# Second layer's down-projection: eight more slots each for split weights and split activations, in the activations' dead tile

## The chip, the cores and the metric

The kernel runs on one core of one Trainium2 chip. The metric is the device time of one execution in microseconds (us). An execution of one program repeats within some tenths of a per cent; the median of a few is given. A profile is taken of one execution more, by the hardware profiler, and has a time of its own.

## The reference, cut to what matters

The program is one inference step of a two-layer encoder for 1152 rows (1024 of a prompt, 128 of eight samples), with d_model 1024. Each layer has attention, and a GEGLU MLP with a causal convolution of width 3 between the up-projection and the activation. What bears on this case is the end of the MLP, in the second layer:

```python
D_MODEL = 1024; D_FF = 2816
def conv_ffn(h, prev, w_up, conv_w, conv_b, w_down):
    u = h @ w_up
    ...
    a, g = jnp.split(y, 2, axis=-1)
    out = (jax.nn.gelu(g) * a) @ w_down      # (1152 x 2816) @ (2816 x 1024)
...
x = layer_norm(ALPHA * x + (1 + g_f) * f, ln_g[l, 1], ln_b[l, 1])
```

All inputs and results are float32.

## The kernel before

**Split operands.** A float32 operand is held as two tiles in the matmul's rounded type: hi, a cast of the value (ScalarE, `copy`, line 183), and lo, the value less hi (VectorE, `split`, line 194). A product is then three matmuls: lo by hi, hi by lo, hi by hi. A pair (hi, lo) lives in a slot; `Ring` hands the slots of a list out in turn, again and again. Before a slot is written anew, the last matmul that read it must be done.

**The second layer's down-projection** is `down2`, called at the end of `ffn` (for the first layer `down` is called in its place, which is not touched). The 22 blocks of 128 rows of the weight are taken as 11 pairs, m = 0 to 10, the even block e = 2m and the odd block o = 2m + 1. The prompt's product is computed by a scheme of Strassen's kind with seven block products in place of eight, in the order 1, 2, 5, 6, 3, 7, 4. Sums of activation blocks (`actS`) and of weight blocks (`wT`) were written to DRAM during the up-projection, the activations themselves to `actD`. `product(q, banks, ...)` runs one of the seven: for each m it calls `fetch`, which gives an activation (hi, lo) and a weight (hi, lo), and issues 4 x 3 matmuls (128 x 128 by 128 x 512, line 1603) into four banks of PSUM. In products 1, 2, 5 and 6 there are three more for the 128 sample rows into a bank of their own, so a step has 15 matmuls there and 12 in products 3, 7 and 4.

What `fetch` issues for a step:

- the activation (`act`): a load of 128 x 512 (line 1595), in products 1, 2, 5 and 6 another of 128 x 128 for the samples (line 1597), into the lo half of its slot; then the cast and the subtraction in place;
- the weight (`weight`): a load of 128 x 512 (line 1587) into a raw buffer, or, for `wT`, straight into the lo half of its slot; then cast and subtraction;
- product 5 loads two weight blocks (lines 1628 and 1629), takes their difference on GpSimd (line 1630) and splits both, so it takes two weight slots per step; product 6 too takes two, one for `wT` and one for a raw weight.

Raw buffers are rings of their own: nine (`early`) in products 1 and 2, six (`late`) in the others, eight (`diffs`) in product 5.

**The slots.** The weights' ring `subs` has six slots of 512 columns, halves of the tiles `wh` and `wl`. The activations' ring `acts` has seven slots of 640 columns in `X1` (named `xa` in the profile). `H` is a tile of 128 x 2 x 8 x 1152 (hi and lo, eight blocks of d_model, 1152 rows) which holds the up-projection's split activations; after the last matmul of the up-projection (line 1229) nobody reads them. Before the change, eight slots in H (columns 512 to 1024 of each block, `more`) join the weights' ring after product 6, for products 3, 7 and 4, and for product 4 the ring starts over at its first slot.

**Between the products** the banks are read out: by ScalarE copies (line 1722 after product 1, 1729 after product 5) and VectorE additions (1732 after product 6, 1749, 1756), with gates by line 1657. Product 2 adds on in product 1's banks, product 6 in product 5's, product 3 in product 6's. Meanwhile residual rows, gates and LN rows are loaded (1081, 970, 971, 978), and the rows' normalisation (`head`, `tail`, `norm_last`, lines 1001 to 1026) follows product 6 and runs to the end. The last six steps of product 4 are kept back (`KEEP`) and run bank by bank, so that the last rows can be finished one after another.

**Order.** No engine's order is written by hand. A planner runs through the program with simulated times and puts onto each engine's queue what is ready, earlier program lines first. All loads and stores are issued by SyncE's one queue (SP), in the planner's order. An instruction on the chip waits for the tiles it needs, and each engine's queue is worked off in order.

Of the kernel before, what the change touches and what calls it, by code (L numbers as in the profile page):

```python
# [36 lines left out]
NK = NFF // 2  # L37
# [68 lines left out]
class Trunk:  # L106
# [285 lines left out]
    def attention(self, l, wk):  # L392
# [5 lines left out]
        if l == 0:  # L398
            self.X1 = self.x1p.tile([128, 9216], F32R, name="xa", tag="x1")
        xa = Arena(self.X1)  # L400
        khi = [xa.take(1024) for _ in range(2)]
# [683 lines left out]
    def woload(self, l, i):  # L1085
        X1, X2 = self.X1, self.X2
        loc = ((5120, 6144), (7168, 8192), (0, 2048), (3072, 1024))
        loc = [tuple(X1[:, o : o + 1024] for o in p) for p in loc]
        loc = self.wslots[0:2] + loc + [self.wslots[2], (X1[:, 4096:5120], X2[:, 0:1024])]
        self.wo[i] = self.wload(self.I[("wo0", "wo1")[l]][i // 4, i % 4], el="ppppvvvv"[i], dst=loc[i])  # L1090
        return self.wo[i]
# [60 lines left out]
    def tviews(self):  # L1152
        X1, X2 = self.X1, self.X2
        TT = [(X1[:, 0:2304], X1[:, 2304:4608]), (X1[:, 4608:6912], X1[:, 6912:9216]), (X2[:, 0:2304], X2[:, 2304:4608])]
        return [[x.rearrange("p (k n) -> p k n", k=4) for x in t] for t in TT]
# [390 lines left out]
    def down2(self, l, xsrc, xdst, affs, act_sums):  # L1546
        nc, I, F, H = self.nc, self.I, self.F, self.H
# [26 lines left out]
        late = Ring(raws)  # L1574
        diffs = Ring([F[:, o : o + 512] for o in range(2048, 6144, 512)])
        subs = self.subslots(ws[1:4])
        X1 = self.X1
        acts = Ring([(X1[:, o : o + 640], X1[:, o + 640 : o + 1280]) for o in range(0, 8960, 1280)])
        more = [(H[:, 0, c, 512:1024], H[:, 1, c, 512:1024]) for c in range(8)]
        hfr = Ring([self.hf, self.gateS])  # L1580
        wdn, wT, actD, actS = I["wdn"][l], self.wT, self.actD, self.actS
        lo_half, hi_half = slice(0, 512), slice(512, 1024)
# [62 lines left out]
        def product(q, banks, bs=None, new=True, keep=0, hook=None):  # L1645
            for m in range(NK - keep):
                a, w, w2 = fetch(q, m)
                for i in range(4):
                    mm(self.bank(banks[i]), a, i, w, new and m == 0, m == NK - 1)
                if bs is not None:  # L1650
                    mm(self.bank(bs), a, 4, w2, q in (1, 5) and m == 0, q in (2, 6) and m == NK - 1)
                if hook:
                    hook(m)
# [81 lines left out]
        def tails(k):  # L1735
            def hook(m):
                if m in TAILS[k]:
                    t = TAILS[k][m]
                    tail(t)
                    rows(*{0: (3,), 1: (4, 5), 2: (6,), 3: (7,)}.get(t, ()))  # L1740

            return hook

        subs = Ring(subs.items + more)
        rings = Ring([zt]), Ring([self.hf])
        rows(8, 0)
        product(3, B, new=False, hook=tails(0))
# [9 lines left out]
            nc.vector.tensor_sub(q5[i], u4[i], q5[i])  # L1757
            gate(u4[i], u4[i], 4 + i, 1)
        keep = KEEP[l]
        subs = Ring(subs.items[0 : NK - len(more)] + more if l == 0 else subs.items)  # L1760
        product(4, E, keep=keep, hook=tails(2))
        kept = [(m, fetch(4, m)) for m in range(NK - keep, NK)]
        for i in range(4):
# [296 lines left out]
```

## Time and profile before

| | us |
|---|---|
| median of 3 runs | 2764.35 |
| lowest, highest run | 2763.35, 2785.1 |
| profiled execution | 2773.36 |
| its span, from the first to the last instruction | 2771.6 |
| mean granted TensorE clock in it | 0.985 |
| the stage's matmuls (line 1603), first to last start | 2487.7 to 2755.2 |

Times in the profile's rows are us from the start of the span. PE is TensorE's matmuls, PEld its weight loads, DVE VectorE, ACT ScalarE, POOL GpSimd, SP SyncE, which issues the DMAs; a "q" behind the name means the engine's queue. `PS` is PSUM, `wl` and `wh` the weight slots, `xa` the activation slots, `F`, `ws`, `w0f` and `x2f` other tiles in SBUF. A row of a waits view has the engine, line and tile that waited, what it waited for, the total in us, how often, and the longest. A row of a chain has start, length and what was going on. A row of a timeline has start, length, engine, line, operation, tiles and count, and in brackets the engine's idle time just before and what ended it.

### The profile page before, as it was taken

What the parts mean: (1) busy time and instruction counts of PE and PEld (TensorE: products, weight loads), DVE (VectorE), ACT (ScalarE), POOL (GpSimd) and SP (SyncE); (2) the same over time, 40 slices, a digit from 0 to 9 for tenths busy, and PEclk for the clock granted to TensorE, in tenths of its full rate; (3) what the DMA queues carried; (4) which work ended last, traced back from release to release, by engine and by line L of the source; (5) the groups of instructions that cost most, each with busy time, mean ns of one, the idle gap of its engine ahead of it and who ended that gap; (6) DMA issues with size and microseconds to landing.
All of it is one profiled execution on the core that took longest, in us unless ns stands there. A gap on an engine that the chain in (4) does not pass through costs nothing.

```text
span 2771.6 us, 47111 instructions
## 1 busy us (share of the span) xinstructions
PE 2654.1 (96%) x17266; PEld 2347.8 (85%) x17266; DVE 1928.0 (70%) x3836; ACT 1347.6 (49%) x2777; POOL 1063.8 (38%) x775
## 2 busy tenths in 40 slices
PE   7999889999999999999999999989999999999997
PEld 5987768989999998788898888867899999997776
DVE  4376768776667684867754677766787778785669
ACT  3475733433334343443436666663454454454454
POOL 3132523444434467664221121242466656632101
PEclk9999999999999999999999999999999999999999
DMA  8756534574444446765757457763445343347564
GB/s 295 232 160 187 152 105 167 163 238 150 139 157 152 143 140 221 243 213 183 273 199 264 112 164 193 217 203 129 167 139 184 135 143 130 136 152 240 191 222 156
DMA packets 229527, 498.27 MB, mean 180 GB/s; under 512 B 37456, under 2 KB 99232, under 8 KB 229296
## 3 DMA queue, kind: packets, MB, share of 16 engines
q1 hardware_dynamic: 229296, 495.27, 54.8%
q8 instruction: 136, 2.23, 0.3%
q14 instruction: 95, 0.78, 0.1%
HBM read 378.15 MB, written 126.47 MB: 182 GB/s over the span
## 4 chain that ended last, share of the span: by engine, by line
PE 36%; DVE 6%; DMA 4%; issue 2%; ACT 2%; POOL 1%; SPq 0%; DVEq 0%; ACTq 0%; POOLq 0%
PE PS L1229 15%; PE PS L1603 6%; PE PS L325 5%; PE PS L312 4%; PE PS L608 2%; PE PS L586 1%; DVE wl L194 1%; DMA xa<-actD 1%; PE PS L557 1%; DVE F L524 1%; PE PS L560 1%; DVE xa L194 1%; DMA w0f<-in_wdn_dram 1%; PE PS L735 1%; DMA xa<-actS 0%
## 5 line engine op out<-in xcount | busy, mean ns | idle before, releaser
L1229 PE MATMUL PS<-H,wh 128*128 128x256 f32 (+1 forms) x2288 | 351.6, 294 | 0.0
L1229 PEld LDWEIGHTS PS<-H,wh 128*128 128x128 f32 x2288 | 318.5, 189 | 0.4 <-issue 0.4
L1190 DVE TENSOR_TENSOR F<-PS,F 128x256 f32<-128x256 f32 (+1 forms) x446 | 196.9, 452 | 168.0 <-PE PS L1229 160.2
L183 ACT CAST wh<-F 128x512 fp32r<-128x512 f32 (+3 forms) x241 | 147.8, 624 | 214.2 <-PE PS L1229 101.5
L194 DVE TENSOR_TENSOR wl<-F,wh 128x512 fp32r<-128x512 f32 (+2 forms) x225 | 219.6, 987 | 44.3 <-ACT wh L183 42.9
L1229 PE MATMUL PS<-H,wl 128*128 128x256 f32 (+1 forms) x1144 | 201.4, 297 | 6.8 <-ACT F L1197 6.2
L1603 PE MATMUL PS<-wh,xa 128*128 128x512 f32 x584 | 189.2, 403 | 13.7 <-ACT wh L183 7.0
L1229 PEld LDWEIGHTS PS<-H,wl 128*128 128x128 f32 x1144 | 168.4, 189 | 12.9 <-ACT F L1197 6.4
L1229 PE MATMUL PS<-xa,wh 128*128 128x320 f32 (+1 forms) x1152 | 176.2, 294 | 0.0
L183 ACT CAST xa<-xa 128x384 fp32r<-128x384 f32 (+2 forms) x143 | 85.9, 604 | 172.4 <-DMA xa<-actD 143.8
L1229 PEld LDWEIGHTS PS<-xa,wh 128*128 128x128 f32 x1152 | 159.7, 188 | 0.4 <-issue 0.4
L1472 DVE TENSOR_TENSOR xa<-xa 128x384 fp32r<-128x384 f32 x66 | 98.9, 1511 | 77.4 <-ACT xa L183 77.4
L1603 PEld LDWEIGHTS PS<-wh,xa 128*128 128x128 f32 x584 | 112.2, 193 | 42.6 <-ACT wh L183 8.8
L646 POOL TENSOR_TENSOR F<-F,x2r 64x512 f32<-64x512 f32 x62 | 79.3, 1279 | 164.9 <-DVE F L622 149.8
L183 ACT CAST wh<-ws 128x512 fp32r<-128x512 f32 (+1 forms) x131 | 95.5, 736 | 95.1 <-PE PS L1229 40.9
L1349 POOL TENSOR_TENSOR F<-F 128x1152 f32<-128x1152 f32 x44 | 124.2, 2823 | 43.9 <-DVE F L1342 23.6
L325 PE MATMUL PS<-xa,H 128*128 128x512 f32 x504 | 132.5, 405 | 6.2 <-ACT xa L183 3.3
L312 PE MATMUL PS<-H,w0r 128*128 128x384 f32 (+1 forms) x720 | 137.4, 341 | 0.0
L1278 DVE SCALAR_TENSOR_TENSOR F<-F 128x1024 f32<-128x1024 f32 (+2 forms) x160 | 130.1, 863 | 4.3 <-ACT F L1317 3.3
L312 PE MATMUL PS<-H,wh 128*128 128x384 f32 (+1 forms) x672 | 131.3, 339 | 0.0
L586 PE MATMUL PS<-C,F 128*128 128x128 f32 x720 | 112.6, 280 | 14.7 <-DVE wh L593 5.8
L312 PEld LDWEIGHTS PS<-H,w0r 128*128 128x128 f32 x720 | 124.3, 188 | 2.8 <-issue 1.5
(354 smaller groups left out, 6885.9 us busy)
## 6 DMA issues: line engine op xcount, KB each, us to landing
ws<-in_adaw_dram SPq DMA_DIRECT2D x64, 512.0 KB
ws<-in_wup_dram SPq DMA_DIRECT2D x49, 512.0 KB
F<-in_adaw_dram SPq DMA_DIRECT2D x48, 512.0 KB
F<-in_wup_dram SPq DMA_DIRECT2D x39, 512.0 KB
actD<-F SPq DMA_DIRECT2D x33, 576.0 KB
ws<-in_wdn_dram SPq DMA_DIRECT2D x33, 512.0 KB
F<-in_wdn_dram SPq DMA_DIRECT2D x33, 512.0 KB
xa<-kH SPq DMA_DIRECT2D x60, 256.0 KB
```

The costliest lines, as they stand in the source:

```text
L183: nc.scalar.copy(out, in_)
L194: self.eng(el).tensor_sub(lo, src, hi.bitcast(F32))
L312: mm = self.nc.tensor.matmul(out[:, 0:n], w[a][:, k * 128 : k * 128 + 128], H[:, p, k, s0 : s0 + n], start=i == 0, stop=i == 23)
L325: self.nc.tensor.matmul(out[:, 0:n], H[:, p, j * kn + k, t0 : t0 + 128], w[a][:, k * n : k * n + n], start=i == 0, stop=i == 23,)
L586: nc.tensor.transpose(t[:, n * 128 : n * 128 + 128], p[:, (kt - k0) * 128 : (kt - k0) * 128 + 128], self.ident)
L646: self.eng("v" if last else "p").tensor_mul(on[r, q], on[r, q], rb[r, :])
L1190: nc.vector.tensor_add(d, v(ps), a if len(a.shape) == 3 else v(a))
L1229: self.pairmm = nc.tensor.matmul(ps[:, 0:m], w[a][:, k * 128 : k * 128 + 128], x(p, k, n), start=start and c == 0, stop=c == 11, skip_grou ...
L1278: nc.vector.scalar_tensor_tensor(o, u, cw[:, cc, i : i + 1], o, op0=ALU.mult, op1=ALU.add)
L1349: nc.gpsimd.tensor_mul(yg, yg, ya)
L1472: nc.vector.tensor_sub(lo, raw, hi.bitcast(F32))
L1603: self.downmm = nc.tensor.matmul(ps, a[p][:, i * 128 : i * 128 + 128], w[q], start=first and c == 0, stop=last and c == 2, skip_group_chec ...
```

## The change

The eight slots in H are taken from the start of the stage: the weights' ring has 14 slots in all seven products (6 as before, then columns 0 to 512 of each of H's eight blocks), the activations' ring has 15 (7 as before, then columns 512 to 1152 of each block). The two later changes of the weights' ring go: it isn't extended after product 6 and doesn't start over for product 4.

```diff
         subs = self.subslots(ws[1:4])
+        subs = Ring(subs.items + [(H[:, 0, c, 0:512], H[:, 1, c, 0:512]) for c in range(8)])
         X1 = self.X1
-        acts = Ring([(X1[:, o : o + 640], X1[:, o + 640 : o + 1280]) for o in range(0, 8960, 1280)])
-        more = [(H[:, 0, c, 512:1024], H[:, 1, c, 512:1024]) for c in range(8)]
+        acts = [(X1[:, o : o + 640], X1[:, o + 640 : o + 1280]) for o in range(0, 8960, 1280)]
+        acts = Ring(acts + [(H[:, 0, c, 512:1152], H[:, 1, c, 512:1152]) for c in range(8)])
...
-        subs = Ring(subs.items + more)
         rings = Ring([zt]), Ring([self.hf])
         rows(8, 0)
         product(3, B, new=False, hook=tails(0))
...
         keep = KEEP[l]
-        subs = Ring(subs.items[0 : NK - len(more)] + more if l == 0 else subs.items)
         product(4, E, keep=keep, hook=tails(2))
```

## The prediction

> **What bounds the kernel now.** I read the page first, for the engine shares and the chain, then the rows of the stage's one matmul line.
>
> ```profile
> span 2771.6 us, 47111 instructions
> PE 2654.1 (96%) x17266; PEld 2347.8 (85%) x17266; DVE 1928.0 (70%) x3836; ACT 1347.6 (49%) x2777; POOL 1063.8 (38%) x775
> PE 36%; DVE 6%; DMA 4%; issue 2%; ACT 2%; POOL 1%; SPq 0%; DVEq 0%; ACTq 0%; POOLq 0%
> L1603 PE MATMUL PS<-wh,xa x584: 387/394/795, 2487.7 to 2751.8; 128*128 128x512 f32 x195
> L1603 PE MATMUL PS<-wl,xa x292: 388/394/628, 2489.9 to 2751.6; 128*128 128x512 f32 x146
> L1603 PE MATMUL PS<-H,xa x180: 387/389/402, 2681.3 to 2755.2; 128*128 128x512 f32 x180
> ...
> L1229 PE MATMUL PS<-H,wh x2288: 276/304/468, 535.4 to 2494.2; 128*128 128x256 f32 x102, 128*128 128x320 f32 x89
> ```
>
> TensorE is the engine of the chain. In the L1603 rows (count, then shortest, median and longest duration in ns, then first and last start) the stage has 584 + 292 + 180 = 1056 matmuls and lasts from 2487.7 to 2755.2, 267.5 us; before 2681 none of them reads H. The up-projection (L1229) reads H for the last time at 2494.2.
>
> The next view cuts the stage into stretches: length, then busy time and instructions of PE, PEld, DVE, ACT and POOL, granted clock, DMA share, GB/s. I set the cuts where the 10 us rows of the same view had few matmuls.
>
> ```profile
> 2485.00:2500.00 15.00, 12.53 (x63) 9.76 (x63) 12.59 (x24) 10.08 (x19) 1.93 (x3) 1.00 0.66 214
> 2500.00:2530.00 30.00, 30.00 (x133) 24.62 (x132) 20.34 (x20) 10.82 (x18) 14.09 (x9) 1.00 0.95 295
> 2530.00:2545.00 15.00, 11.63 (x40) 8.98 (x39) 5.02 (x7) 7.38 (x13) 0.00 (x0) 0.77 0.60 202
> 2545.00:2605.00 60.00, 60.00 (x259) 48.60 (x258) 36.39 (x45) 24.39 (x40) 9.98 (x7) 1.00 0.57 177
> 2605.00:2640.00 35.00, 28.48 (x113) 21.74 (x112) 19.15 (x30) 19.29 (x34) 0.00 (x0) 0.95 0.59 189
> 2640.00:2660.00 20.00, 20.00 (x89) 16.43 (x88) 10.57 (x17) 9.04 (x16) 0.00 (x0) 1.00 0.60 204
> 2660.00:2670.00 10.00, 7.49 (x26) 5.68 (x26) 9.13 (x16) 5.08 (x9) 0.00 (x0) 0.83 0.51 168
> 2670.00:2750.00 80.00, 80.00 (x352) 65.53 (x351) 68.20 (x136) 42.89 (x70) 5.24 (x2) 1.00 0.64 218
> ```
>
> Undisturbed, 2545 to 2605 holds 259 matmuls in 60 us: 4.32 per us, 0.232 us each. 1056 of them would take 245 us, so the stage holds about 23 us that are not its matmuls (a little of it is the up-projection's last). That is the ceiling of what any buffering can give: 0.8% of the kernel. Three stretches miss matmuls. 2530 to 2545 should hold 64.8 and holds 40: 24.8 missing, **5.7 us**. 2605 to 2640 should hold 151 and holds 113: 38 missing, **8.8 us**. 2660 to 2670 should hold 43 and holds 26: 17 missing, **4.0 us**. Together 18.5 us; the rest, some 4 to 5 us, lies before 2500, in the handover from the up-projection. From 2670 on nothing is missing.
>
> What each of the three waits for is in the waits of each engine and in the chain between 2590 and 2664:
>
> ```profile
> PE PS L1603 <- DVE xa L194: 3.4, 1, 3.4
> PE PS L1603 <- DVE F L1732: 2.5, 1, 2.5
> ...
> 2524.49 0.38 SPq L1597 DMA_DIRECT2D xa<-actD  x1
> 2534.25 0.72 ACT L183 CAST xa<-xa 128x640 fp32r<-128x640 f32 x1 [5.96 <-DMA xa<-actD]
> ...
> 2610.62 4.18 DMA wl<-wT
> 2614.83 0.20 ACT wh L183
> 2618.47 5.18 DMA wl<-wT
> 2623.67 0.63 ACT wh L183
> 2627.96 5.59 DMA xa<-actD
> ...
> 2657.82 3.25 DMA w0f<-in_wdn_dram
> 2661.09 0.63 ACT H L183
> 2661.74 0.56 DVE H L194
> 2662.35 0.69 DVE F L1732
> ```
>
> The first stall is one activation load: issued at 2524.49, cast at 2534.25, 9.8 us later, right behind the 30 us in which DMA was 0.95 busy. The second is a run of loads of 4.2 to 5.6 us, each on the chain from issue to landing. The third is the eviction L1732, queued on DVE behind two splits of weights whose raw load was late.
>
> **The change part by part.** No arithmetic, DMA or matmul is added or taken away; what changes is how early a load or a split may start.
>
> *Weight slots, 6 to 14 in products 1, 2, 5, 6.* Products 5 and 6 use two slots per step of 15 matmuls, so six slots hold three steps: 3 x 15 x 0.232 = 10.4 us from a slot's release to its next use. In product 6 the wT load goes straight into the lo half of its slot and so can't start before the release. In that time must fit the wait on SP, the landing (4.2 to 5.2 us above), the cast and the subtraction, each behind what is queued on ACT and DVE:
>
> ```profile
> L183 ACT CAST xa<-xa 128x640 fp32r<-128x640 f32 x44 | 31.6, 728 | 62.6 <-DMA xa<-actD 51.6 <-PE PS L1603 3.8 <-issue 2.5
> L194 DVE TENSOR_TENSOR xa<-xa 128x640 fp32r<-128x640 f32 x44 | 38.6, 886 | 47.7 <-ACT xa L183 42.1 <-DMA xa<-actD 2.8 <-DMA F<-in_wdn_dram 2.7
> L194 DVE TENSOR_TENSOR wl<-F,wh 128x512 fp32r<-128x512 f32 x37 | 35.0, 968 | 3.5 <-ACT wh L183 3.5
> ```
>
> With 14 slots it is seven steps, 24.4 us. The chain's loads then start some 14 us sooner than they are needed, more than the longest landing in it. Bounds for the second stall: 0 to 8.8 us gone; I take 8, since its waits are short against the 14 us won.
>
> Can DVE follow? A step of product 5 costs it 0.886 + 2 x 0.968 = 2.82 us per 3.48 us of matmuls, and from 2545 to 2605 it was busy 36.39 of 60. It can, and it may begin product 5 while product 2 still runs. ACT is further from its limit.
>
> *Activation slots, 7 to 15.* A slot lasts one step, so the depth goes from 24 to 52 us. The first stall sits where seven slots were already deep enough on paper, so depth alone doesn't explain it: DMA was full at 295 GB/s. What the slots can do is bring loads forward into 2485 to 2500, where DMA was only 0.66 busy: 15 us x 0.34 x 295/0.95 GB/s is 1.6 MB, or five activation loads of 256 + 64 KB. Bounds: 0 to 5.7 us; I take 4.
>
> *The third stall.* No slot is short for L1732 itself. It goes if the two splits ahead of it on DVE have their data earlier. Bounds 0 to 4.0; I take 2.5, nearer to gone, because the loads of product 3 get the same lead as all others.
>
> About 2 us of its 4.0 are slow clock: granted 0.83 in that stretch, with matmuls 0.43 us apart after a wait of only 2.5 us.
>
> ```profile
> 2663.18 0.47 PE L1603 MATMUL PS<-wh,xa 128*128 128x512 f32 x1 [2.51 <-DVE F L1732]
> 2665.81 1.05 PE L1603 MATMUL PS<-wh,xa 128*128 128x512 f32 x2
> 2666.66 0.63 PE L1603 MATMUL PS<-wl,xa 128*128 128x512 f32 x1
> ```
>
> The Trainium skill, "TensorE: Matmul & The Clock Gate", in Part 1 on the HAM clock gate, puts the fall to half clock at an idle window of about 3.4 us; by that a 2.5 us wait should cost 2.5 us and not the 4.0 counted above, and the sum would be 1 to 1.5 us smaller. The spacing in the last two rows speaks against it here.
>
> *The new wait, and the start.* A load into H waits on SP for the up-projection's last matmul on that block; behind it in SP's one queue stand the first weights of product 1, and TensorE waits for those. Today's kernel has that wait too, for three loads of product 7, which now come later:
>
> ```profile
> 2493.78 1.32 SPq L1587 DMA_DIRECT2D H<-wT  x3
> ```
>
> They were issued within a microsecond of the block's release, 6 us after the stage's first matmul, so I count the wait itself at nothing; what it costs if it is misplaced is a rival below. The first six weights and seven activations lie where they lay, so the 4 to 5 us before 2500 stay. Splits of the later ones no longer wait for a matmul and can slip in between the last up-projection's evictions, where DVE is busy 12.59 of 15 us. Bounds: one split per engine lost twice, 2 us, down to nothing; I take 1 us lost.
>
> *Products 3, 7, 4.* They had 14 weight slots; they get no more. The last product's ring now runs on instead of starting over. Nothing is missing there after 2670, so I count 0. DVE hides this: 68.20 of 80 us busy. If the matmuls came faster than before, DVE would be late next, but they can't.
>
> **Sum:** 8 + 4 + 2.5 - 1 = 13.5 us. The profiled execution took 2773.36 us (span 2771.6, and 1.8 around it); it would become 2759.9. The median of the runs is 2764.35, 9 us lower for the same work, so the forecast is 2764.35 - 13.5 = **2751 us**.
>
> **The rivals.**
>
> *Slots were not the limit.* SP's longest waits between 2485 and 2663 are not for matmuls:
>
> ```profile
> SPq L1587 <- DVE wl L194: 37.5, 18, 5.8
> SPq L1628 <- DVE wl L194: 17.1, 6, 4.5
> SPq L1595 <- PE PS L1603: 13.1, 17, 3.8
> ```
>
> L1587 and L1628 wait for raw buffers (rings of 6, 9 and 8), which the change leaves alone; only 13.1 us are loads waiting for a matmul to free a slot. If raw buffers and transfers rule, only the wT loads gain, about 5 us: 2759. Against it: a raw buffer is freed by the split, and the split waited for a slot.
>
> *A burst at the start.* Eight further activation loads are 8 x 320 KB = 2.56 MB, at 295 GB/s 8.7 us; issued ahead of the first weights they make these late by that, plus 2 us of slow clock. Net 13.5 - 10.7: 2761. The Trainium skill, "DMA: Bandwidth & Descriptors", section on queues, rings and completion order, says that each DMA engine takes descriptors in ring order, and so speaks for this; the load of 9.8 us behind full DMA agrees. Against it: H comes free only when the first seven activation loads are out.
>
> *Slower: splits ahead of evictions.* ACT and DVE run in order. With more slots the planner may place splits of far-ahead steps in front of the evictions at the six ends of products. If such a split's load is late, ACT or DVE stands (6 us once, at 2534), the banks stay full, and TensorE stops: 6 + 2 us of slow clock each, against one such place today (4.0 us). From two places on the gain is gone; at three, the likeliest, 24 - 13.5 = 10.5 slower: 2775; at all six, 2799.
>
> **How the numbers follow.** Forecast, 8 to 18.5 us gained (2746 to 2756): 0.55. All three stalls and part of the start too (2738 to 2746): 0.08. Slots not the limit (2756 to 2763): 0.17. Burst (2758 to 2766): 0.07. Splits ahead of evictions (2766 to 2799): 0.13. The range 2742 to 2768 leaves out about 0.04 below and 0.12 above. One per cent, 27.6 us, is about what a measurement of this kernel can tell from no change, and it is more than the 23 us that the stage holds. So faster by over 1% needs gains outside the count: 0.03. Slower by over 1% needs five or six late evictions: 0.06. Within 1%: 0.91.
>
> **What would show it.** In the changed profile, casts and subtractions write H from about 2490 on, and matmuls read weights and activations from it in product 1. Right: 2605 to 2640 at 4.3 matmuls per us with no wT load on the chain; fewer waits of casts for activation loads; the last matmul near 2742. Wrong: the same waits with later landings (raw buffers, burst), or TensorE waiting for L1722, L1729 or L1732 at the end of products (the slower rival), or a new gap before 2500.

## The result, and the profile after

The changed kernel takes 2762.3 us (median of 14 runs, 2753.53 to 2766.88) against 2770.43 us for the kernel before (14 runs, 2763.35 to 2785.1). The ratio is 0.9971 with a 95% interval of 0.9959 to 0.9983: about 8 us faster, where 13.5 us were forecast. The interval leaves out both no change and the forecast's ratio (0.9951).

From the page of after, and from its stage matmuls grouped by shape (the matmul line is now 1604, one lower down than before):

```profile
span 2753.7 us, 47055 instructions
L1604 PE MATMUL PS<-wh,xa x220: 387/392/792, 2481.1 to 2737.8; 128*128 128x512 f32 x110
L1604 PE MATMUL PS<-H,xa x177: 389/389/398, 2514.3 to 2737.1; 128*128 128x512 f32 x177
```

The stage's 1056 matmuls now start between 2481.1 and 2737.8: 256.7 us, where they took 267.5. The profiled execution is 17.9 us shorter than the one before, but some 8 us of that lie ahead of the stage, in work that the change does not touch (the first L1229 matmul starts at 523.5, and at 531.6 before). So only the stage is compared below.

The stretches of after, with the columns explained in the prediction:

```profile
2480.00:2490.00 10.00, 3.30 (x12) 2.10 (x12) 10.00 (x17) 7.62 (x15) 0.00 (x0) 0.92 0.88 289
2490.00:2500.00 10.00, 8.60 (x28) 7.17 (x29) 7.40 (x14) 6.03 (x10) 2.37 (x4) 0.56 0.90 289
...
2530.00:2545.00 15.00, 14.40 (x64) 11.48 (x63) 8.04 (x11) 9.60 (x16) 1.30 (x1) 1.00 0.68 226
...
2605.00:2640.00 35.00, 34.02 (x149) 27.51 (x148) 19.57 (x32) 19.26 (x35) 0.00 (x0) 1.00 0.64 208
...
2660.00:2670.00 10.00, 10.00 (x45) 8.24 (x44) 6.63 (x11) 3.65 (x7) 0.00 (x0) 1.00 0.82 239
```

The three stretches that missed matmuls are nearly full: 64 for 40, 149 for 113, 45 for 26. But the start has a hole: 12 matmuls in ten microseconds with VectorE busy for all ten, and then a granted clock of 0.56.

TensorE's timeline around the last twelve matmuls of the up-projection, first of after, then of before:

```profile
2490.69 1.19 PE L1229 MATMUL PS<-H,wl 128*128 128x256 f32 x4 [5.23 <-ACT PS L1340]
2491.69 1.91 PE L1229 MATMUL PS<-H,wh 128*128 128x256 f32 x8
```

```profile
2492.80 0.71 PE L1229 MATMUL PS<-H,wl 128*128 128x256 f32 x4 [0.59 <-DVE F L1334]
2493.35 1.10 PE L1229 MATMUL PS<-H,wh 128*128 128x256 f32 x8
```

TensorE stands 5.23 us where it stood 0.59, and the eight matmuls behind take 1.91 us for 1.10: the slow clock (a granted clock of 0.56 above) comes on top.

A table puts all kernels side by side. A loss is what the gap between the starts of neighbouring matmuls exceeds 0.231 us by (0.107 us for the up-projection's last), summed by place from the trace. "Start" runs up to 2510, "1 to 2" is the handover from product 1 to 2, "weights" the stretch 2590 to 2660, in products 5 and 6, where before waits for weights; before's third stall, at 2663, is among "other". The last column is the measured ratio less one, times the median of before in the same measurement.

| kernel | start | 1 to 2 | weights | other | sum | sum against before | ratio, 95% | measured us |
|---|---|---|---|---|---|---|---|---|
| before | 3.9 | 6.1 | 9.4 | 4.3 | 23.7 | | 1 | |
| after | 13.1 | 0.9 | 1.3 | 1.0 | 16.3 | -7.4 | 0.9971, 0.9959 to 0.9983 | -8.0 |
| hold_both | 11.8 | 7.0 | 1.5 | 1.4 | 21.7 | -2.0 | 1.0004, 0.9991 to 1.0016 | +1.1 |
| hold_dve | 11.9 | 6.6 | 1.2 | 0.4 | 20.1 | -3.6 | 0.9998, 0.9983 to 1.0012 | -0.6 |
| acts_only | 10.9 | 0 | 8.0 | 0.6 | 19.5 | -4.2 | 0.9990, 0.9976 to 1.0003 | -2.8 |
| subs_only | 9.9 | 6.6 | 0 | 4.8 | 21.3 | -2.4 | 0.9994, 0.9979 to 1.0009 | -1.7 |
| near_hold | 4.8 | 0 | 0 | 4.8 | 9.6 | -14.1 | 0.9936, 0.9915 to 0.9956 | -17.7 |
| near_evict | 3.7 | 0 | 1.6 | 0.3 | 5.6 | -18.1 | 0.9939, 0.9919 to 0.9959 | -16.9 |
| evict_after | 14.0 | 0 | 1.8 | 0.2 | 16.0 | -7.7 | 0.9967, 0.9955 to 0.9979 | -9.1 |
| evict_before | 3.5 | 4.4 | 8.7 | 5.6 | 22.2 | -1.5 | 0.9997, 0.9982 to 1.0011 | -0.8 |
| near_subs | 4.0 | 0 | 0 | 4.8 | 8.8 | -14.9 | 0.9956, 0.9940 to 0.9971 | -12.2 |
| near_acts | 6.8 | 0 | 7.8 | 0.4 | 15.0 | -8.7 | 0.9975, 0.9961 to 0.9990 | -6.9 |

The sums come from one profiled execution each, the ratios from five rounds; they agree within 4 us. The sums count waits alone. Between them the matmuls came a little faster too: the mean distance of starts that lie 200 to 260 ns apart is 228.4 ns in after and 230.2 in before, which over 1056 matmuls is another 1.9 us. Matmuls with their weight in H had 228.0 ns in before already, those with it in `wh` 230.6; why, no run here shows.

### The profile page after: what moved, and what is told of

Same layout as the page of the kernel before. It is cut to its first block, busy times and chain, and to the rows that moved or that the text cites. A ratio compares the mean times of both kernels' runs of the same rounds, so it can differ in the third digit from the quotient of the medians.

```text
span 2753.7 us, 47055 instructions
## 1 busy us (share of the span) xinstructions
PE 2642.9 (96%) x17266; PEld 2342.1 (85%) x17266; DVE 1924.2 (70%) x3836; ACT 1346.8 (49%) x2777; POOL 1066.5 (39%) x775
## 4 chain that ended last, share of the span: by engine, by line
PE 36%; DVE 7%; DMA 3%; issue 2%; ACT 2%; POOL 1%; SPq 0%; DVEq 0%; ACTq 0%; POOLq 0%
PE PS L1229 14%; PE PS L1604 7%; PE PS L325 5%; PE PS L312 4%; PE PS L608 2%; PE PS L586 1%; PE PS L557 1%; DVE wl L194 1%; DVE F L524 1%; DMA w0f<-in_wdn_dram 1%; PE PS L560 1%; DVE xa L194 1%; PE PS L735 1%; DMA H<-actD 0%; DVE x2r L593 0%
## 5 line engine op out<-in xcount | busy, mean ns | idle before, releaser
L1229 PE MATMUL PS<-H,wh 128*128 128x256 f32 (+1 forms) x2288 | 352.8, 295 | 0.0
L1229 PEld LDWEIGHTS PS<-H,wh 128*128 128x128 f32 x2288 | 319.7, 189 | 0.4 <-issue 0.4
L183 ACT CAST wh<-F 128x512 fp32r<-128x512 f32 (+3 forms) x224 | 137.8, 625 | 209.7 <-PE PS L1229 94.1
L194 DVE TENSOR_TENSOR wl<-F,wh 128x512 fp32r<-128x512 f32 (+2 forms) x208 | 199.3, 968 | 42.3 <-ACT wh L183 41.7
L1229 PE MATMUL PS<-H,wl 128*128 128x256 f32 (+1 forms) x1144 | 201.8, 297 | 13.0 <-ACT F L1197 6.3
L1229 PEld LDWEIGHTS PS<-H,wl 128*128 128x128 f32 x1144 | 168.9, 190 | 19.0 <-ACT F L1197 6.5
L1229 PE MATMUL PS<-xa,wh 128*128 128x320 f32 (+1 forms) x1152 | 176.2, 294 | 0.0
L1229 PEld LDWEIGHTS PS<-xa,wh 128*128 128x128 f32 x1152 | 159.7, 188 | 0.4 <-issue 0.4
L183 ACT CAST wh<-ws 128x512 fp32r<-128x512 f32 (+1 forms) x120 | 88.9, 747 | 96.0 <-PE PS L1229 39.9
L1278 DVE SCALAR_TENSOR_TENSOR F<-F 128x1024 f32<-128x1024 f32 (+2 forms) x160 | 130.1, 863 | 4.4 <-ACT F L1317 3.1
L194 POOL TENSOR_TENSOR wl<-ws,wh 128x1024 fp32r<-128x1024 f32 x28 | 73.1, 2610 | 134.1 <-ACT wh L183 104.0
L325 PEld LDWEIGHTS PS<-xa,H 128*128 128x128 f32 x504 | 95.2, 192 | 28.6 <-ACT xa L183 3.8
L524 DVE CUSTOM_DVE_ANT_0 F<-PS,F,C 128x256 f32<-128x256 f32 (+3 forms) x208 | 97.4, 479 | 30.5 <-PE PS L560 15.0
```

The lines of the kernel that those rows point to most:

```text
L183: nc.scalar.copy(out, in_)
L194: self.eng(el).tensor_sub(lo, src, hi.bitcast(F32))
L325: self.nc.tensor.matmul(out[:, 0:n], H[:, p, j * kn + k, t0 : t0 + 128], w[a][:, k * n : k * n + n], start=i == 0, stop=i == 23,)
L524: nc.vector.tensor_tensor_reduce(out=p[:, c0 : c0 + w], in0=ps, in1=b, scale=1.0, scalar=init, op0=ALU.add, op1=ALU.min, accum_out=nm)
L1229: self.pairmm = nc.tensor.matmul(ps[:, 0:m], w[a][:, k * 128 : k * 128 + 128], x(p, k, n), start=start and c == 0, stop=c == 11, skip_grou ...
L1278: nc.vector.scalar_tensor_tensor(o, u, cw[:, cc, i : i + 1], o, op0=ALU.mult, op1=ALU.add)
```

## The experiments

**What stands at the start.** VectorE's timeline of after, while TensorE waits:

```profile
2484.72 0.75 DVE L1278 SCALAR_TENSOR_TENSOR PS<-F,PS 128x512 f32<-128x512 f32 x1
2485.38 1.56 DVE L194 TENSOR_TENSOR H<-H 128x640 fp32r<-128x640 f32 x2
2486.85 0.69 DVE L194 TENSOR_TENSOR H<-ws,H 128x512 fp32r<-128x512 f32 x1
2487.45 1.00 DVE L1278 SCALAR_TENSOR_TENSOR PS<-F,PS 128x112 f32<-128x112 f32 x2
2488.35 0.69 DVE L194 TENSOR_TENSOR H<-ws,H 128x512 fp32r<-128x512 f32 x1
2488.95 0.74 DVE L1342 SCALAR_TENSOR_TENSOR F<-F,PS 128x512 f32<-128x512 f32 x1
2489.61 0.69 DVE L194 TENSOR_TENSOR H<-w0f,H 128x512 fp32r<-128x512 f32 x1
2490.21 0.34 DVE L1334 SCALAR_TENSOR_TENSOR F<-F,PS 128x120 f32<-128x120 f32 x1
```

The releaser that the wait of 5.23 us names is on ScalarE, but it had itself waited for VectorE:

```profile
2489.79 0.78 ACT L1340 ACTIVATE PS<-F 128x512 f32<-128x512 f32 x1 [0.70 <-DVE F L1342]
```

L1278, L1334, L1340 and L1342 are steps of the convolution, which uses the PSUM banks that the last twelve up-projection matmuls need. Five splits into H (2 x 0.78 + 3 x 0.69 us) stand between its instructions. They belong to steps that TensorE reaches after 2514 (the first matmul with a weight in H, the row `PS<-H,xa` above, starts at 2514.3). Before the change such splits had no slot and could not be there. That gave two theories. *Theory 1, order*: the new slots let splits of far-off steps onto the in-order queues of ScalarE and VectorE, in front of what TensorE needs next. *Theory 2, loads*: the new loads, issued early, fill the DMA queues (share 0.88 and 0.90 between 2480 and 2500, 0.73 and 0.70 before) and make the first weights late.

**hold_both**: after, with the sixteen splits of the first round through H (weights 7 to 14, activations 8 to 15) queued behind the convolution's last gate row: on ScalarE behind its first activation, on VectorE behind its L1334. The loads stay as early as in after.

```diff
+            if gg:
+                self.rowend = {"a": a.ins, "v": v.ins}   # the row's first activation, and L1334
...
-            self.split(raw, hi, lo, "a", "v")
+            with held("w"):                              # weights 7 to 14, acts 8 to 15
+                self.split(raw, hi, lo, "a", "v")        # issue_after(self.rowend[e]) for e in "av"
```

> The changed kernel, with the first splits into H (weights 7 to 14, activations 8 to 15 of the stage) queued on ScalarE and on VectorE behind the last gate row of the convolution (its first activation and its line 1334); their loads stay as early as in the changed kernel. Theory 1 (the far-ahead splits, in front of that row on the two queues, hold up the up-projection's last twelve matmuls): TensorE's wait of 5.2 us ahead of these falls to 1 us or less, the slow clock behind it goes, the stretch from the twelve matmuls before to the end of the span falls from 274.5 us to 265 to 268, and the time is 15 to 19 us below the kernel before (ratio 0.993 to 0.9945). Theory 2 (the eight early activation loads, in front of the first weights in the DMA rings, make the start late): the wait and the slow clock stay, ratio about 0.997 as in the changed kernel.

It gained nothing: 1.0004, where theory 1 had expected 0.993 to 0.9945. TensorE's timeline of hold_both, and part of ScalarE's:

```profile
2496.75 0.71 PE L1229 MATMUL PS<-H,wl 128*128 128x256 f32 x4 [0.61 <-DVE F L1334]
2502.19 2.07 PE L1618 MATMUL PS<-wh,xa 128*128 128x512 f32 x4 [3.79 <-ACT wh L183]
2506.06 0.79 PE L1618 MATMUL PS<-wl,xa 128*128 128x512 f32 x1 [1.80 <-DVE wl L194]
```

```profile
2497.48 1.35 ACT L183 CAST H<-H 128x640 fp32r<-128x640 f32 x2
2498.74 1.65 ACT L183 CAST H<-ws 128x512 fp32r<-128x512 f32 x3
2500.30 0.77 ACT L1342 ACTIVATE PS<-F 128x512 f32<-128x512 f32 x1
2501.02 0.60 ACT L183 CAST H<-w0f 128x512 fp32r<-128x512 f32 x1
2501.52 0.61 ACT L183 CAST wh<-w0f 128x512 fp32r<-128x512 f32 x1
```

The wait for the convolution is back at 0.61 us. But the released splits now stand in front of a further activation of the convolution (L1342 here) and of the second weight's cast (`wh<-w0f`, 2501.52), for which TensorE waits 3.79 us, and then 1.80 for its subtraction. The loss moved by one place in the same queues. And a stall that after no longer had is back: 7.0 us at the handover from product 1 to 2.

**hold_dve**: the same with VectorE's subtractions alone held back.

```diff
-                for e in "av": es.enter_context(self.tc.issue_after(self.rowend[e]))
+                for e in "v": es.enter_context(self.tc.issue_after(self.rowend[e]))
```

> As the kernel held on both engines, but held on VectorE alone: the casts into H may still stand in front of the gate row on ScalarE. Theory 1 with VectorE as the place (seven subtractions, 5.3 us, stand between the mark and line 1334): nearly all comes back, wait 1.5 us or less, ratio 0.993 to 0.995. Theory 1 with ScalarE as the place (the first activation of line 1340 was 2.5 us late): 2 to 3 us of the wait stay, ratio 0.995 to 0.996. Theory 2: as the changed kernel, 0.997.

0.9998, with the same two losses (11.9 and 6.6 us); 0.993 to 0.995 had been expected. The wait for the convolution is gone: the twelve matmuls start at 2490.91, right behind the ones before, although casts into H still stand in front of its instructions on ScalarE. So VectorE's queue was the place of that wait. In its stead TensorE waits longest for the second weight's subtraction, in front of which eleven splits into H now stand on VectorE (from 2490.67 on):

```profile
2500.24 0.80 PE L1618 MATMUL PS<-wl,xa 128*128 128x512 f32 x1 [5.09 <-DVE wl L194]
```

**acts_only and subs_only**: one kind of slot alone.

```diff
 acts_only, on before:
-        acts = Ring([...seven slots...])
+        acts = Ring([...seven slots...] + [(H[:, 0, c, 512:1152], H[:, 1, c, 512:1152]) for c in range(8)])
 subs_only, on after:
-        acts = Ring(acts + [(H[:, 0, c, 512:1152], H[:, 1, c, 512:1152]) for c in range(8)])
+        acts = Ring(acts)                       # seven slots, as before
```

> The kernel before with the activations' fifteen slots alone; the weights' ring as before (six slots, eight in H after product 6). Theory 1: five splits into H stand in front of line 1334, so the wait is 2 to 4 us; the first stall of before (5.7 us, near 2530) goes, the second (8.8 us, 2605 to 2640) stays at 7 or more since it is the six weight slots', so the time is within 5 us of the kernel before (ratio 0.998 to 1.001). Rival (activation slots are what the second stall lacked too): second stall gone, ratio 0.996 or less.

> The changed kernel with the activations' seven slots of before; the weights' ring with fourteen. Theory 1: seven splits into H in front of line 1334, three of them early, so the wait is 2 to 4 us; the second and the third stall of before go (12 us), the first stays (5.7 us): ratio 0.996 to 0.998. Rival (activation slots were what the second stall lacked): second stall stays at 5 us or more, ratio 0.999 or above.

Neither gives a gain that stands clear of no change (0.9990, 0.9994). The table says why: each clears its own stalls and each has the start's loss of 10 to 11 us. The weights' stretch keeps 8.0 us with activation slots alone and loses nothing with weight slots alone. So the weight slots clear the second stall, and either kind clears the third. (The 4.8 us under "other" of subs_only are in the main a new wait, 3.5 us for gate L1657 behind product 2.) For subs_only 0.996 to 0.998 had been expected: the start took more than was thought.

**The first stall, read anew.** The 6.1 us at 2536 of before, where product 1 hands over to product 2, had been read as one late activation. TensorE's row there, VectorE's subtraction of that activation, and ScalarE's rows just behind the cast of 2534.25 that waited 5.96 us for its load:

```profile
2535.89 1.22 PE L1603 MATMUL PS<-wh,xa 128*128 128x512 f32 x2 [3.37 <-DVE xa L194]
```

```profile
2535.01 0.82 DVE L194 TENSOR_TENSOR xa<-xa 128x640 fp32r<-128x640 f32 x1 [5.78 <-ACT xa L183]
```

```profile
2534.88 0.61 ACT L183 CAST wh<-F 128x512 fp32r<-128x512 f32 x1
2535.40 0.58 ACT L1722 COPY x2f<-PS 128x512 f32<-128x512 f32 x1
2535.88 1.06 ACT L1674 ACTIVATE F<-F 128x1024 f32<-128x1024 f32 x1
2536.84 1.55 ACT L1722 COPY x2f<-PS 128x512 f32<-128x512 f32 x3
```

TensorE restarts at 2535.89, right behind the subtraction, which ends at 2535.83. The first copy L1722 ends at 2535.98, later than that. So in before TensorE did wait for the late activation, as the prediction had it. By count the waiting matmul is the stage's 175th: product 1 has 11 x 15 = 165, and nine of product 2 ran ahead of any copy, so these must be those of the sample rows, whose bank is not read out there.

But product 2 can't go on past its sample rows until copies L1722 have emptied product 1's banks, and the copies stood on ScalarE behind the same cast: the first came only 0.1 us after the activation. hold_both, with all slots in place, shows the copies alone as what TensorE waits for, ScalarE first, then TensorE:

```profile
2544.76 0.73 ACT L183 CAST xa<-xa 128x640 fp32r<-128x640 f32 x1 [5.72 <-DMA xa<-actD]
...
2549.60 1.54 ACT L1737 COPY x2f<-PS 128x512 f32<-128x512 f32 x3
```

```profile
2550.21 6.10 PE L1618 MATMUL PS<-H 128*128 128x512 f32 x16 [4.60 <-ACT x2f L1737]
```

Left out between the two ScalarE rows are three more casts, one of which waits 1.36 us for its load, and the scaling of a residual row. hold_dve and subs_only wait for the same copies, 3.9 and 2.6 us.

So *theory 3*: theory 1's rule holds at the ends of products too. Casts of later steps, some waiting for their loads, stand in front of an eviction. That this cost after only 0.9 us was put down to the 13 us lost at the start, which had given the loads time to land. If so, mending the start alone brings the handover's stall back, and both have to be mended together. (hold_both, with 11.8 us lost at the start and 7.0 at the handover, already speaks against that part.)

**near_hold**: the sixteen splits are queued behind the second weight's cast and subtraction in place of the convolution row.

```diff
+                if own["w"] == 4:                        # the second weight
+                    late2.append(nc.scalar.copy(hi, raw).ins)
+                    late2.append(nc.vector.tensor_sub(lo, raw, hi.bitcast(F32)).ins)
...
+            with held("w"):                              # issue_after(i) for i in late2
```

> The first of the two orders alone (H's first splits behind the second weight's split). Theory 3: the start loses 4 us in place of 13, but then TensorE reaches the handover to product 2 some 9 us sooner and waits there for the copies behind a cast of product 5, 6 to 7 us: from the mark to the end 271 to 274 us, ratio 0.996 to 0.9975. If the handover's stall is not of the queue, it stays at 1 us and the ratio is 0.993 to 0.995. Theory 2: start as before, 13 us.

**near_evict**: near_hold, and the casts of product 2's fetches from its fourth step on and of all of product 5's are queued on ScalarE behind the last of the four copies after product 1 (each pass of the loop sets `read1` anew). **evict_after** and **evict_before** put this second edit alone on after and on before.

```diff
+            self.read1 = nc.scalar.copy(p1[i], self.bank(A[i])).ins
...
+                    if q == 2 and m >= 3 or q == 5:
+                        es.enter_context(self.tc.issue_after(self.read1))
                     a, w, w2 = fetch(q, m)
```

> The changed kernel with two orders added: the first splits into H queued on ScalarE and VectorE behind the split of the stage's second weight, and the casts of product 2 from its fourth step on and of product 5 queued on ScalarE behind the four copies (line 1722 before) that empty product 1's banks. Theory 3 (in-order queues: splits for far-off steps stand in front of the split or eviction that TensorE waits for next; more slots only let more of them stand there): the start loses 4 us in place of 13, the handover from product 1 to 2 loses 1 or less, the rest stays as in the changed kernel; from the mark to the end 266 to 269 us in place of 274.5, ratio to before 0.9930 to 0.9950. Theory 2 (early loads clog DMA, so the near operands themselves are late): start and handover still lose 8 us or more between them, ratio 0.996 or above.

> The second of the two orders alone, on the changed kernel. Theory 3: nothing to win but the 0.9 us that the handover still loses, since the start's 13 us come first and cover it: ratio within 0.001 of the changed kernel's 0.9971. If it gains 4 us or more, the start's loss is not what covered it.

> The second of the two orders alone, on the kernel before: no slot is added. Theory 3: the stall at the handover (5.7 us, 2530 to 2545) was ScalarE's queue, a cast of product 2's fourth step in front of the copies, so it falls to 1.5 us or less without any slot; the others stay: ratio 0.9975 to 0.999. The prediction's reading (TensorE waits for that activation itself, late for want of slots or of DMA): the stall stays at 4 us or more, ratio 0.9995 to 1.001.

near_hold, 0.9936, and near_evict, 0.9939, are faster than both kernels (the upper end of near_evict's interval just touches the lower end of after's, 0.9959); their own intervals overlap almost wholly. The stretches of near_hold at the start:

```profile
2480.00:2490.00 10.00, 8.58 (x41) 6.76 (x40) 9.48 (x17) 7.24 (x13) 0.22 (x1) 0.83 0.87 295
2490.00:2500.00 10.00, 9.29 (x47) 7.64 (x45) 9.33 (x13) 9.39 (x18) 1.53 (x1) 1.00 0.85 280
```

DMA is as busy as in after (0.87 and 0.85), yet 88 matmuls run in these 20 us for 40, and the start loses 4.8 us for 13.1. The eight activation loads into H are issued as early, too: 4.3 to 0.3 us before the matmuls ahead of the last twelve end, against 4.7 to 0.7 us in after. So theory 2 falls as the cause of the start's loss, and the order of the queues, which the edit changed, is left.

The expectation that near_hold's handover from 1 to 2 would lose 6 to 7 us was missed: it lost nothing, as its expectation had put down for the case that the handover's stall is not of the queue. The casts in front of the copies had their loads in time, so the run does not tell queue from load there. But with it the supposition falls that the start's loss had covered the handover: hold_both and hold_dve lost much at the start (11.8 and 11.9 us) and much at the handover (7.0 and 6.6), near_hold little at the one and nothing at the other. Why after lost only 0.9 us there stays open. What came instead was a stall one handover further on, product 2 to 5, where gate L1675 (line 1657 of before) reads the banks. VectorE's timeline of near_hold, then TensorE's:

```profile
2568.72 0.83 DVE L194 TENSOR_TENSOR xa<-xa 128x640 fp32r<-128x640 f32 x1 [2.11 <-ACT xa L183]
2569.46 0.68 DVE L1675 TENSOR_TENSOR x2f<-PS,F 128x512 f32<-128x512 f32 x1
```

```profile
2570.20 5.99 PE L1621 MATMUL PS<-H 128*128 128x512 f32 x18 [2.96 <-DVE x2f L1675]
```

The same picture on the other engine: a subtraction that waits for a late activation stands in front of an eviction, which is late by as much. With slow clock it cost 4.8 us. In near_evict it isn't there, and that kernel's losses are the lowest of all, 5.6 us, although its measured time is no better than near_hold's.

evict_after got rid of the 0.9 us at the handover and kept the start's 14.0, as theory 3 says. evict_before was a miss for theory 3: 4.4 us were left at the handover, where at most 1.5 were expected, and both this and the ratio of 0.9997 lie where the prediction's reading had put them. But TensorE's wait there, 2.6 us, is for copy L1725 and no longer for the activation. ScalarE's timeline of evict_before:

```profile
2528.91 0.59 ACT L1725 COPY x2f<-PS 128x512 f32<-128x512 f32 x1
2536.33 1.06 ACT L1677 ACTIVATE F<-F 128x1024 f32<-128x1024 f32 x1 [6.83 <-issue]
2537.29 1.54 ACT L1725 COPY x2f<-PS 128x512 f32<-128x512 f32 x3
```

The first copy is early, at 2528.91; but the scaling of a residual row (L1677) stands in front of the other three, and ScalarE stood 6.83 us ahead of it. In before it has the same place (L1674, at 2535.88 above), without a wait of its own: there the late cast may have hidden it. That it waited for that row's load, which is the tile it reads, is an inference: the view names no releaser. With the casts out of the way another instruction that waits held up the copies, so this run shows again that an eviction can be late by the queue, and not that the casts' order alone made the stall of before.

**near_subs and near_acts**: what each kind of slot is worth once the start's order is kept: subs_only and acts_only with near_hold's edit, applied to the splits that go into H.

```diff
 near_subs, on subs_only:
+            with held("w"): ...                         # weights 7 to 14 behind the second weight's split
 near_acts, on acts_only:
+            with held("a"): ...                         # activations 8 to 15, likewise
```

> Only the eight further weight slots, with the splits of weights 7 to 14 issued behind the second weight's cast and subtraction; the activations keep seven slots. It asks what each kind of slot is worth once the queues' order at the start is kept. If the order is what cost the 5 to 6 us more at the start with weight slots alone, the start loses 4 us as before in place of 9.9, and the stall at 2610 (9.4 us lost before) stays away: ratio 0.995 to 0.997 if the handover from product 1 to 2 still loses 6 us, since activations have no more slots. If weight slots are worth nothing by themselves, as their run of 0.9994 reads, the ratio stays within 0.9985 to 1.001.

> Only the eight further activation slots, with the splits of activations 8 to 15 issued behind the second weight's cast and subtraction; the weights keep six slots until product 6. If the order at the start is what took their gain (0.9990), the start loses 4 us in place of 10.9, the handover from product 1 to 2 loses nothing or comes back with up to 6 us, and the stretch 2600 to 2656 keeps its 8 us: ratio 0.996 to 0.9985. If both kinds are needed together, 0.9985 to 1.001.

0.9956 and 0.9975, both within what was expected, though near_subs lost nothing at the handover, where 6 us had been put down. Weight slots alone are worth 12 us and activation slots alone 7 us, where without the order they gave 1.7 and 2.8. Together that would be 19, and near_hold measured 17.7. TensorE's waits, first of near_subs, then of near_acts:

```profile
PE PS L1619 <- DVE xa L194: 2.6, 1, 2.6
```

```profile
PE PS L1622 <- ACT wh L183: 4.4, 4, 1.7
PE PS L1622 <- ACT wh L1603: 2.7, 1, 2.7
```

Each still waits for the kind that it has too few slots for: near_subs for an activation (at 2517, 4.5 us with slow clock), near_acts for weights (four waits, 4.4 us; 7.8 us lost in the weights' stretch). near_acts' 2.7 us is the start again: the second weight's cast there stands behind casts of product 7's early `wT` weights, which this edit does not hold back.

## Why the prediction was right or wrong

**The base.** The forecast stood on the median of three runs, 2764.35; fourteen runs gave 2770.43. The profiled execution of before, 2773.36, was nearer to that, and the text had noted the 9 us between them. Of the 11.3 us between forecast and result, 6.1 are this, a choice of base and no mechanism; the rest is the gain, 8 us for 13.5.

**The sum, term by term** (losses of before less losses of after):

| term | forecast | in the traces |
|---|---|---|
| second stall, 2605 to 2640 | 8 | 9.4 - 1.3 = 8.1 |
| first stall, 2530 to 2545 | 4 | 6.1 - 0.9 = 5.2 |
| third stall, 2660 to 2670 | 2.5 | 4.3 - 0 = 4.3 |
| products 3, 7, 4 | 0 | -1.0 (2711) |
| the start | -1, bounds -2 to 0 | 3.9 - 13.1 = -9.2 |
| sum | 13.5 | 7.4 |

The faster matmuls (1.9 us, above) are not in it; the prediction had said that matmuls can't come faster.

**The step that failed is the start's.** "One split per engine lost twice" was to be the most, since H was read until 2494.2 and splits into it were expected "from about 2490 on". H is not freed at once. These rows, grouped by shape, are ScalarE's casts into H in after up to 2500:

```profile
L183 ACT CAST H<-H x7: 710/725/728, 2479.8 to 2498.7; 128x640 fp32r<-128x640 f32 x7
L183 ACT CAST H<-F x3: 615/616/617, 2473.5 to 2474.5; 128x512 fp32r<-128x512 f32 x3
```

The first is at 2473.5, 20 us ahead of the last matmul that reads H: a slot comes free with its own block. Up to sixteen slots that come free ahead of the stage, with loads that land one after another, put one split after another onto engines that at that moment feed TensorE's next matmuls. The "new gap before 2500", which the prediction had named as a sign of being wrong, came. The row that could have told it was in the prediction, "DVE is busy 12.59 of 15 us" with 24 instructions at the start: an engine with a sixth of its time free can't take on eight subtractions of 0.69 to 0.82 us unless something is put off. By these rows the 2 us should have been up to 8 x 0.75 = 6 us of splits on VectorE, an estimate, plus the slow clock.

**Right for the reason given:** the second stall. With 14 weight slots it is gone, with six it stays (acts_only), and no `wT` load is on the chain any more. The chain of after in that stretch (the 1.0 us that TensorE still waits there is copy L1730, behind the cast of the activation whose load is the second row):

```profile
2589.87 16.33 PE PS L1604 x72
2606.20 4.71 DMA xa<-actS
...
2612.09 51.95 PE PS L1604 x226
```

**About right in size, with half of the reason:** the first stall, 5.2 us for 4. TensorE did wait for the late activation in before, and in the two kernels with activation slots alone (acts_only, near_acts) nothing is lost there. But the copies out of product 1's banks stood behind the same cast, and the prediction counted no such wait: in hold_both and hold_dve, with all slots in place, they cost 7.0 and 6.6 us. Why after lost only 0.9 us there stays open, so that the size came out near the forecast is in part luck.

**The third stall** went wholly, as its upper bound had it; the 2.5 us taken were too few by 1.8. There too VectorE's eviction L1732 had stood behind two splits.

**The rivals.** "Splits ahead of evictions" named the mechanism, but looked for it at the six ends of products at a price for each; it struck at the start, at the convolution's last row in the stage before, and it moved from place to place when one was mended (hold_both, near_hold). It took 9.2 us off the gain and did not reach the slower side. "A burst at the start" put the same loss, 10.7 us, in the same place for another cause, and near_hold's busy DMA and equally early loads with no such loss speak against it. "Slots were not the limit" falls: with the order kept, slots bring 12, 7 and 17.7 us.

The Trainium skill, "Perfetto Trace Analysis", section "Optimization Strategy", says that consistent bubbles can mean too little room for the next tile. The trace agrees for the second stall (8.0 us with six weight slots, none with fourteen). It does not for the first: a stall at its place came back with all slots there (7.0 us in hold_both).

## What to carry to other kernels

A free buffer is a licence to run ahead, and an in-order engine that runs ahead does far-off work in front of near work. When slots are added, ask which instructions they let into each queue, at the places where that engine also empties PSUM or prepares the very next operand, and hold the far-off ones behind the near ones: here the slots alone brought 8 us, and the slots with that order about 17. When a stall's releaser is a load or a split, look at what else stands behind it on the same engine, since TensorE may need that next.

## What had not been expected of the hardware

Short waits, too, were followed by half clock. near_hold at the start, TensorE's timeline, and the stretch as a whole:

```profile
2484.25 0.74 PE L1621 MATMUL PS<-wh,xa 128*128 128x512 f32 x2 [1.05 <-ACT wh L183]
2485.26 0.49 PE L1621 MATMUL PS<-wh,xa 128*128 128x512 f32 x1 [0.27 <-DVE F L1190]
...
2486.36 0.63 PE L1621 MATMUL PS<-wh,xa 128*128 128x512 f32 x1
2486.79 0.63 PE L1621 MATMUL PS<-wl,xa 128*128 128x512 f32 x1
```

```profile
2486.00:2490.00 4.00, 4.00 (x13) 3.19 (x14) 3.99 (x8) 2.19 (x5) 0.22 (x1) 0.58 0.65 228
```

After waits of 1.05 and 0.27 us the matmuls start 0.43 us apart at a granted clock of 0.58. The Trainium skill, "TensorE: Matmul & The Clock Gate", Part 1 on the HAM clock gate, gives half clock after an idle window of about 3.4 us; here the row shows it after waits far shorter. What in this stretch set it off stays open. Before, the same place had waits of 0.23 and 0.85 us and kept the full clock (1.00 from 2485 to 2500), so a stall's price can't be told from its length alone.
